# Issuing the second mixing stage of a two-layer trunk in emission order

## The chip, the cores and the metric

One core of a Trainium2 chip runs the kernel. The time is device microseconds of one execution, the median of several; the profile is of one execution more, taken by the hardware profiler.

## What is computed

A trunk of two layers over 272 positions (16 learned ones ahead of 256 of the input) with 2048 features, in float32. Each layer mixes over positions and then runs a gated feed-forward block; a norm ends it.

```python
for layer in range(DEPTH):
    hn = rmsnorm(h, norm_mix_g[layer])
    if layer % 2 == 0:      # linear recurrence + differential attention
        mix = jnp.concatenate([ya, yb], axis=-1) @ ev_w_out[j]
    else:                   # state-space layer + RWKV-7 time mixing
        u, dcols = z[..., :S5_WIDTH], z[..., S5_WIDTH:]
        mix = jnp.concatenate([yc, yd], axis=-1) @ od_w_out[j]
    h = h + mix
    h = h + swiglu(rmsnorm(h, norm_ffn_g[layer]), ...)
return rmsnorm(h, final_norm_g)[:, N_META:]
```

The change touches the second layer's mixing. Its RWKV-7 part is a recurrence over positions in 16 heads of 64 features: per position the state is decayed, corrected by a rank-one term and extended by a new one. The kernel computes it in blocks of 64 positions, two heads at a time (a pair), and needs per block the inverse of triangular matrices of 16 x 16.

## The kernel before

**The dense stream.** All weights are read once, as pieces of up to 8 chunks of 128 x 128. `load_piece_` (line 209) takes a buffer `st` of the pool `wst` (three buffers), starts its load on the sync queue, lets ScalarE cast it to `hi` (line 215) and VectorE compute the rest `lo` (line 216); `whi` and `wlo` have three buffers each. `run_dense` (line 218) walks over the items; each has one or two pieces, an optional `pre`, and an `evac` that empties its PSUM bank. Ahead of a piece's matmuls it emits load and casts of the piece two further on (`ahead=2`). A chunk is three matmuls (lines 249 to 251): `hi` with `xhi`, `hi` with `xlo`, `lo` with `xhi`. After each chunk it calls `tick` (line 104).

**Background work.** `tick` counts chunk steps and advances generators: `s5_states` (the state-space part, one of 32 steps each 13 chunk steps or so, with eight instructions on VectorE), and the pairs of heads, `rwkv` (line 1064). Each `yield n` lets n chunk steps pass before the next part is emitted; all between two yields is emitted in one go. A pair runs in two halves, divided by a bare `yield`: the first prepares its factors and the inverse, the second uses them. Two pairs are under way at most, one in each half: the first half of the next pair starts when the second half of this one has. `rw_finish` emits a pair's remaining parts at once where a later one would overtake its buffers.

**The second mixing stage** is `mix1_items` (line 927): 36 projections of 16 chunks, then the gate of the state-space part (8 items of 8), and the output projection in three passes (16 x 8, 16 x 4, 16 x 4): 896 chunk steps. Projections come per pair as key, receptance, value and one of the state-space input. Their `evac` calls `shift` (line 902): GpSimd clears the first column of `zs` (line 907), VectorE empties the bank into the other columns (line 261), ScalarE scales into `ze` (line 909), and VectorE combines both (line 910). `zs` has two buffers, `ze` one; the state-space input also writes both, and four stores per projection carry them to `s5u`.

**The inverse** in `rwkv`. ScalarE's queue issues the store of the blocks `ld` and later, right ahead of line 1193, four loads `ls` (line 1191) that gather the 16 x 16 blocks. GpSimd inverts them: two clears, then a loop of 15 rounds with a product into `xt` (line 1200) and a sum into `xs` (line 1202). ScalarE's queue issues four stores to `xd` (line 1205) and one load `d16` (line 1207). Loads, inverse and stores are emitted in one go; `yield 34` follows.

**Norm factors.** `head_factors` (line 1291) sums squares with small matmuls (line 1297), scales on VectorE (line 1299), takes a power on GpSimd (line 1300) and spreads the result by a copy on VectorE (line 1302); after a `yield` of 9 (first half) or 8 (second) two or four matmuls (line 1306) use it.

**The order before.** Program order is not issue order: a list scheduler places each instruction on its engine at compile time, by simulated times, taking of those that are ready the one emitted first; casts and evacuations count as 4000 instructions earlier (`hi_pri`). On the chip each engine then keeps that order.

Of the kernel before, what the change touches and what calls it, by code (L numbers as in the profile page):

```python
# [92 lines left out]
class Net:  # L93
# [73 lines left out]
    def setup(self):  # L167
        nc = self.nc
        self.cp = self.pool("cp", 1)
        self.wst = self.pool("wst", 3)  # L170
        self.whi = self.pool("whi", 3)
        self.wlo = self.pool("wlo", 3)
        self.nt = self.pool("nt", 1)
        self.nt2 = self.pool("nt2", 2)
        self.dr = self.pool("dr", 2, space=bass.MemoryType.DRAM)
        self.pd = self.pool("pd", 2, space=bass.MemoryType.PSUM)
        self.bg = self.pool("bg", 1, space=bass.MemoryType.PSUM)
        cp = self.cp
        self.h = self.t(cp, [128, KC, T], "h")
        self.xhi = self.t(cp, [128, KC, T], "xhi", F32R)  # L180
        self.xlo = self.t(cp, [128, KC, T], "xlo", F32R)
        self.vec = self.t(cp, [128, NV], "vec")
        self.ones = self.t(cp, [128, 1], "ones")
        nc.vector.memset(self.ones, 1.0)
# [727 lines left out]
    def mix1_items(self):  # L912
        nc = self.nc
        I = self.I
        st = {}
# [5 lines left out]

        def open_pools():
            es = st["es"] = ExitStack()
            pl = self.m1 = self.pool("m1", 1, es)
            self.m1b = self.pool("m1b", 2, es)
            self.rw = self.load_const("rw", pl)
            V = nc.vector
            self.omu = self.t(pl, [128, 28], "omu")
            V.tensor_scalar(self.omu, self.v("mu"), -1.0, 1.0, op0=ALU.mult, op1=ALU.add)
            self.hv = self.t(pl, [128, 4, 8], "hv")  # L930
            for i, n in enumerate(("w0", "a0", "ka", "glu_b")):
                V.tensor_scalar(self.hv[:, i], self.v(n), 0.5, None, op0=ALU.mult)
            self.oka = self.t(pl, [128, 8], "oka")
            V.tensor_scalar(self.oka, self.v("ka"), -0.5, 1.0, op0=ALU.mult, op1=ALU.add)
            self.lora = {n: self.t(pl, [128, T], "lo_" + n) for n in ("w", "a", "g0", "g1")}
            st["u"] = self.t(pl, [128, 8, T], "u")
            st["y32"] = self.t(pl, [128, 8, TR], "y32")
            st["es2"] = ExitStack()
            self.m2 = self.pool("m2", 1, st["es2"])
            self.m2b = self.pool("m2b", 2, st["es2"])  # L940
            pl = self.m2
            self.ri = [self.t(pl, [128, 4, 2, 64], f"ri{i}") for i in range(2)]
            self.bk = self.t(pl, [128, 5, 3, 64], "bk")
            nc.gpsimd.tensor_copy(self.bk[:, :, 2], self.rw["ist"].unsqueeze(1).to_broadcast([128, 5, 64]))
            for m in self.ri:
                nc.gpsimd.tensor_copy(m[:, :, 1], self.rw["ist"].unsqueeze(1).to_broadcast([128, 4, 64]))
# [43 lines left out]

        def yd_last():
            self.rw_finish(False, 7)
            st["es2"].close()
            pl = self.pool("m3", 1, st["es"])
            st["yd"] = [self.t(pl, [128, 8 - YA, TR], "yd" + n, F32R) for n in "hl"]
            for c in range(YA, 8):
                self.split(st["yd"][0][:, c - YA], st["yd"][1][:, c - YA], st["y32"][:, c])
# [66 lines left out]
    def rwkv(self, p, x, yd):  # L1064
        nc = self.nc
# [69 lines left out]
        def heads(out, lhs, rhs, start=True, stop=True):  # L1135
            for h in range(2):
                e = slice(64 * h, 64 * h + 64)
                PE.matmul(out[e], lhs[e], rhs[e], start=start, stop=stop)  # L1138
# [9 lines left out]
        st = rw["st"]  # L1148
# [41 lines left out]
        for b in range(4):  # L1190
            nc.scalar.dma_start(ls[10 * b:10 * b + 10], bass.AP(tensor=ld.tensor, offset=ld.offset + 1040 * b,
                                                              ap=[[4096, 10], [64, 16], [1, 16]]))
        xs = self.t(pl, [40, 16, 16], "xs")
        xt = self.t(pl, [40, 16, 16], "xt")
        G.memset(xs, 0.0)
        G.memset(F(xs)[:, 0:256:17], 1.0)
        for s in range(15):
            j, n = s + 1, 15 - s
            o = xt[:, :j, :n]
            G.tensor_tensor(o, ls[:, s + 1:, s].unsqueeze(1).to_broadcast([40, j, n]),  # L1200
                            xs[:, :j, s:s + 1].to_broadcast([40, j, n]), op=M)
            G.tensor_tensor(xs[:, :j, s + 1:], xs[:, :j, s + 1:], o, op=A)  # L1202
        xd = self.dr.tile([10, 4, 256], F32, tag="xd", name="xd")
        for b in range(4):
            nc.scalar.dma_start(xd[:, b], F(xs[10 * b:10 * b + 10]))
        d16 = self.t(pl, [128, 5, 16], "d16")
        nc.scalar.dma_start(d16, bass.AP(tensor=xd.tensor, offset=xd.offset, ap=[[16, 128], [2048, 5], [1, 16]]))
        yield 34
        yield
        lg = self.t(pl, [128, 2, 128], "lg")  # L1210
        nc.sync.dma_start(lg, self.I["w_lora"][p, :, 2:4])
# [45 lines left out]
        for c in range(4):  # L1257
            stt = self.t(pb, [128, 64], "stt")
            o = 256 + 64 * (c % 2)
            S.activation(stt, q[:, o:o + 64], AF.Copy, scale=pc[:, c:c + 1])  # L1260
            yield 2
            if c < 3:
                o = 576 - o
                heads(q[:, o:o + 64], kq[:, c, 1], vb[:, c + 1], True, False)
                heads(q[:, o:o + 64], ma[:, c, 1], stt, False, True)
            o = 64 * c
            heads(q[:, o:o + 64], vb[:, c + 1], kq[:, c, 0], True, False)
            heads(q[:, o:o + 64], stt, ma[:, c, 0], False, True)
        ys = self.t(pl, [128, TR], "ys")
        yield 1  # L1270
        S.copy(ys, q[:, :TR])
        yield 2

        q = self.ps("e")
        PE.matmul(q[:, :TR], rw["cen"], ys, start=True, stop=True)
        sq = self.t(pl, [128, 4, 2, 64], "ma").rearrange("p a b c -> p (a b c)")
        S.activation(sq[:, :TR], q[:, :TR], AF.Square)
        S.activation(ys, q[:, :TR], AF.Copy, scale=self.v("ln_w", p))
        yield 3
        yield from self.head_factors(sq[:, :TR], TR, 1.0 / 64, 64e-5, A, "e",  # L1280
                                     self.t(pl, [128, 2, 128], "ie2"), "iv2", 8)
        o = yd[:, p]
# [159 lines left out]
```

## Time and profile before

| | us |
|---|---|
| median of 3 runs | 2596.49 |
| lowest, highest | 2596.41, 2600.54 |
| the profiled execution | 2599.46 |
| its span, first to last instruction | 2597.7 |
| TensorE busy in it | 2519.6 |
| VectorE busy | 1677.8 |
| ScalarE busy | 1167.0 |
| GpSimd busy | 446.4 |

The stages follow each other in the span: the first mixing up to about 420 us, its feed-forward block up to 1240, the second mixing from 1240 to 1812, its feed-forward block and the output. In the profile PE is TensorE, PEld its weight loads, DVE VectorE, ACT ScalarE, POOL GpSimd; L1202 is line 1202. A tile's name stands without its buffer's number. A matmul's duration overlaps the next one's start, so the pace is read from counts over time, not from durations. The share of the clock that is granted is a mean over a stretch: 1.00 is the upper level, 2.4 GHz, and 0.50 the lower, 1.2 GHz.

### The profile page before, as it was taken

To read this page: it belongs to the slowest core of one execution; us is meant where nothing else is said; L and a number is where in the kernel's file an instruction comes from. 1 tells how busy PE (TensorE), PEld (TensorE's weight loads), DVE (VectorE), ACT (ScalarE), POOL (GpSimd) and SP (SyncE) were. 2 spreads that over 40 slices of the span, in tenths; PEclk is the share of its full clock that TensorE was granted. 3 is DMA by queue.
4 is the path that set the end of the run, shared out by engine and by line. 5 is a ranking of instruction groups with operands and counts; after the bars stand their busy time and mean duration, and the time that the engine had idled before them with its cause. 6 is when DMAs were issued, how large, how long until landed. Compare 5 with 4: busy or idle time off the path is not lost.

```text
span 2597.7 us, 52298 instructions
## 1 busy us (share of the span) xinstructions
PE 2519.6 (97%) x21152; PEld 2445.9 (94%) x21152; DVE 1677.8 (65%) x2716; ACT 1167.0 (45%) x1983; POOL 446.4 (17%) x660
## 2 busy tenths in 40 slices
PE   7999999999999999999998999999999999999997
PEld 7999999999999999999887888789999999999997
DVE  7666868787555555557788888656655555555555
ACT  5555646488333333335433333434544434343434
POOL 3111302100001010102133333520210101010103
PEclk9999999999999999999999999999999999999999
DMA  5444456767655555555554544334565566555654
GB/s 188 141 146 141 151 175 202 227 216 254 207 176 173 175 175 172 177 172 184 183 165 137 160 143 139 91 115 147 171 187 180 186 187 187 187 185 184 185 187 145
DMA packets 164546, 448.41 MB, mean 173 GB/s; under 512 B 39313, under 2 KB 55377, under 8 KB 164049
## 3 DMA queue, kind: packets, MB, share of 16 engines
q1 hardware_dynamic: 147728, 442.77, 54.4%
q10 hardware_dynamic: 16576, 2.30, 0.5%
q8 instruction: 167, 2.74, 0.4%
q14 instruction: 75, 0.61, 0.1%
HBM read 422.14 MB, written 22.87 MB: 171 GB/s over the span
## 4 chain that ended last, share of the span: by engine, by line
PE 81%; DVE 5%; DMA 5%; POOL 4%; issue 2%; ACT 1%; ACTq 1%; SPq 0%; DVEq 0%; POOLq 0%
PE p L251 25%; PE p L249 25%; PE p L250 25%; POOL xt L1200 2%; POOL xs L1202 2%; DVE lo L216 2%; DMA ld<-lf 1%; PE b L1138 1%; DMA s5u<-ze 1%; DMA ls<-ld 1%; ACT hi L215 1%; PE a L519 1%; DVE xlo L275 0%; PE c L548 0%; PE a L1138 0%
## 5 line engine op out<-in xcount | busy, mean ns | idle before, releaser
L215 ACT CAST hi<-st 128x1024 fp32r<-128x1024 f32 (+1 forms) x776 | 793.2, 1023 | 1129.9 <-PE p L250 767.6
L216 DVE TENSOR_TENSOR lo<-st,hi 128x1024 fp32r<-128x1024 f32 (+1 forms) x776 | 929.9, 1199 | 521.0 <-ACT hi L215 517.3
L249 PE MATMUL p<-xhi,hi 128*128 128x272 f32 (+1 forms) x4256 | 1236.5, 291 | 15.0 <-ACT hi L215 11.2
L251 PE MATMUL p<-xhi,lo 128*128 128x272 f32 (+1 forms) x4256 | 1235.2, 290 | 8.6 <-DVE lo L216 8.4
L250 PE MATMUL p<-xlo,hi 128*128 128x272 f32 (+1 forms) x4256 | 1231.9, 289 | 0.0
L249 PEld LDWEIGHTS p<-xhi,hi 128*128 128x128 f32 x4256 | 811.5, 191 | 26.1 <-ACT hi L215 13.2
L251 PEld LDWEIGHTS p<-xhi,lo 128*128 128x128 f32 x4256 | 811.7, 191 | 18.7 <-DVE lo L216 10.7
L250 PEld LDWEIGHTS p<-xlo,hi 128*128 128x128 f32 x4256 | 809.9, 190 | 4.5 <-issue 2.4
L251 PE MATMUL p<-ah,lo 128*128 128x272 f32 (+1 forms) x1408 | 401.9, 285 | 0.4 <-DVE lo L216 0.4
L249 PE MATMUL p<-ah,hi 128*128 128x272 f32 (+1 forms) x1408 | 401.0, 285 | 0.4 <-ACT hi L215 0.4
L250 PE MATMUL p<-al,hi 128*128 128x272 f32 (+1 forms) x1408 | 400.9, 285 | 0.0
L356 POOL TENSOR_TENSOR ga<-ga,rb 128x272 f32<-128x272 f32 (+1 forms) x88 | 127.6, 1450 | 1226.6 <-ACT ga L355 1226.6
L251 PEld LDWEIGHTS p<-ah,lo 128*128 128x128 f32 x1408 | 265.8, 189 | 0.7 <-DVE lo L216 0.7
L249 PEld LDWEIGHTS p<-ah,hi 128*128 128x128 f32 x1408 | 265.6, 189 | 0.7 <-ACT hi L215 0.7
L250 PEld LDWEIGHTS p<-al,hi 128*128 128x128 f32 x1408 | 264.8, 188 | 0.0
L265 DVE TENSOR_TENSOR h<-p,h 128x256 f32<-128x256 f32 (+1 forms) x272 | 117.0, 430 | 135.8 <-PE p L251 134.6
L302 POOL TENSOR_TENSOR acc<-acc,sq 128x272 f32<-128x272 f32 (+1 forms) x56 | 59.5, 1063 | 268.8 <-ACT sq L297 268.3
L365 DVE TENSOR_TENSOR gu<-p,ga 128x272 f32<-128x272 f32 (+1 forms) x88 | 38.1, 433 | 61.2 <-PE p L251 58.3
L354 DVE TENSOR_TENSOR ga<-p,rb 128x272 f32<-128x272 f32 (+1 forms) x88 | 38.1, 432 | 51.9 <-PE p L251 51.4
L1200 POOL TENSOR_TENSOR xt<-ls,xs 40x15 f32<-40x15 f32 (+7 forms) x120 | 52.5, 438 | 57.1 <-DMA ls<-ld 48.5
L275 DVE SCALAR_TENSOR_TENSOR xlo<-h,vec,xhi 128x272 fp32r<-128x272 f32 (+1 forms) x64 | 52.1, 823 | 0.3 <-ACT xhi L274 0.3
L1202 POOL TENSOR_TENSOR xs<-xs,xt 40x15 f32<-40x15 f32 (+7 forms) x120 | 47.6, 397 | 8.8
(357 smaller groups left out, 2268.8 us busy)
## 6 DMA issues: line engine op xcount, KB each, us to landing
st<-in_w_gate SPq DMA_DIRECT2D x176, 512.0 KB
st<-in_w_up SPq DMA_DIRECT2D x176, 512.0 KB
st<-in_w_down SPq DMA_DIRECT2D x160, 512.0 KB
st<-in_w_ev_in SPq DMA_DIRECT2D x80, 512.0 KB
st<-in_w_od_in SPq DMA_DIRECT2D x72, 512.0 KB
st<-in_w_ev_out SPq DMA_DIRECT2D x32, 512.0 KB
stab<-s5p SPq DMA_DIRECT2D x32, 400.0 KB
s5p<-stb SPq DMA_DIRECT2D x8, 1088.0 KB
```

The lines of the kernel that those rows point to most:

```text
L215: nc.scalar.copy(hi[:, :kc], st[:, :kc])
L216: nc.vector.tensor_tensor(lo[:, :kc], st[:, :kc], hi[:, :kc].bitcast(F32), op=ALU.subtract)
L249: nc.tensor.matmul(p[:, :n], hi[:, o + k], xa, start=kk == 0, stop=False)
L250: nc.tensor.matmul(p[:, :n], hi[:, o + k], xb, start=False, stop=False)
L251: nc.tensor.matmul(p[:, :n], lo[:, o + k], xa, start=False, stop=kk == tot - 1)
L265: self.nc.vector.tensor_tensor(self.h[:, m, c0:], p, self.h[:, m, c0:], op=ALU.add)
L275: nc.vector.scalar_tensor_tensor(lo, src, g, hi.bitcast(F32), op0=ALU.mult, op1=ALU.subtract)
L302: nc.gpsimd.tensor_tensor(self.acc[:, c0:], self.acc[:, c0:], sq[:, c0:], op=ALU.add)
L354: nc.vector.tensor_tensor(a[:, :n], p, self.rb[:, :n], op=ALU.mult)
L356: nc.gpsimd.tensor_tensor(a[:, :n], a[:, :n], self.rb[:, :n], op=ALU.mult)
L1200: G.tensor_tensor(o, ls[:, s + 1:, s].unsqueeze(1).to_broadcast([40, j, n]), xs[:, :j, s:s + 1].to_broadcast([40, j, n]), op=M)
L1202: G.tensor_tensor(xs[:, :j, s + 1:], xs[:, :j, s + 1:], o, op=A)
```

## The change

`open_pools`, run ahead of the first projection, opens a region in which TensorE, VectorE, ScalarE and GpSimd each issue their instructions in the order in which the program emits them, the DMA issues on ScalarE's queue with them. `yd_last`, run ahead of the last pass of the output projection, closes it. The sync queue, and the order across engines, stay with the scheduler. In `rwkv` the loads of the blocks, the inverse, the stores and the load of `d16` are now emitted 4, 23 and 4 chunk steps apart, with 4 behind (35 in place of 34), and some yields of the second half grow from 2 or 3 to 4. The pool of incoming weights gets a fourth buffer.

```diff
--- before.py
+++ after.py
@@ -167,7 +167,7 @@
     def setup(self):
         nc = self.nc
         self.cp = self.pool("cp", 1)
-        self.wst = self.pool("wst", 3)
+        self.wst = self.pool("wst", 4)
         self.whi = self.pool("whi", 3)
         self.wlo = self.pool("wlo", 3)
         self.nt = self.pool("nt", 1)
@@ -921,6 +921,8 @@
 
         def open_pools():
             es = st["es"] = ExitStack()
+            st["order"] = self.tc.manual_schedule(engines={nc.tensor.engine, nc.vector.engine, nc.scalar.engine, nc.gpsimd.engine})
+            st["order"].__enter__()
             pl = self.m1 = self.pool("m1", 1, es)
             self.m1b = self.pool("m1b", 2, es)
             self.rw = self.load_const("rw", pl)
@@ -990,6 +992,7 @@
 
         def yd_last():
             self.rw_finish(False, 7)
+            st["order"].__exit__(None, None, None)
             st["es2"].close()
             pl = self.pool("m3", 1, st["es"])
             st["yd"] = [self.t(pl, [128, 8 - YA, TR], "yd" + n, F32R) for n in "hl"]
@@ -1190,6 +1193,7 @@
         for b in range(4):
             nc.scalar.dma_start(ls[10 * b:10 * b + 10], bass.AP(tensor=ld.tensor, offset=ld.offset + 1040 * b,
                                                               ap=[[4096, 10], [64, 16], [1, 16]]))
+        yield 4
         xs = self.t(pl, [40, 16, 16], "xs")
         xt = self.t(pl, [40, 16, 16], "xt")
         G.memset(xs, 0.0)
@@ -1200,12 +1204,14 @@
             G.tensor_tensor(o, ls[:, s + 1:, s].unsqueeze(1).to_broadcast([40, j, n]),
                             xs[:, :j, s:s + 1].to_broadcast([40, j, n]), op=M)
             G.tensor_tensor(xs[:, :j, s + 1:], xs[:, :j, s + 1:], o, op=A)
+        yield 23
         xd = self.dr.tile([10, 4, 256], F32, tag="xd", name="xd")
         for b in range(4):
             nc.scalar.dma_start(xd[:, b], F(xs[10 * b:10 * b + 10]))
+        yield 4
         d16 = self.t(pl, [128, 5, 16], "d16")
         nc.scalar.dma_start(d16, bass.AP(tensor=xd.tensor, offset=xd.offset, ap=[[16, 128], [2048, 5], [1, 16]]))
-        yield 34
+        yield 4
         yield
         lg = self.t(pl, [128, 2, 128], "lg")
         nc.sync.dma_start(lg, self.I["w_lora"][p, :, 2:4])
@@ -1258,7 +1264,7 @@
             stt = self.t(pb, [128, 64], "stt")
             o = 256 + 64 * (c % 2)
             S.activation(stt, q[:, o:o + 64], AF.Copy, scale=pc[:, c:c + 1])
-            yield 2
+            yield 4
             if c < 3:
                 o = 576 - o
                 heads(q[:, o:o + 64], kq[:, c, 1], vb[:, c + 1], True, False)
@@ -1269,14 +1275,14 @@
         ys = self.t(pl, [128, TR], "ys")
         yield 1
         S.copy(ys, q[:, :TR])
-        yield 2
+        yield 4
 
         q = self.ps("e")
         PE.matmul(q[:, :TR], rw["cen"], ys, start=True, stop=True)
         sq = self.t(pl, [128, 4, 2, 64], "ma").rearrange("p a b c -> p (a b c)")
         S.activation(sq[:, :TR], q[:, :TR], AF.Square)
         S.activation(ys, q[:, :TR], AF.Copy, scale=self.v("ln_w", p))
-        yield 3
+        yield 4
         yield from self.head_factors(sq[:, :TR], TR, 1.0 / 64, 64e-5, A, "e",
                                      self.t(pl, [128, 2, 128], "ie2"), "iv2", 8)
         o = yd[:, p]
```

## Rows read from the trace of the kernel before

**Rows 1.** page section 1: busy us (share of the span) x instructions, all engines

```profile
PE 2519.6 (97%) x21152; PEld 2445.9 (94%) x21152; DVE 1677.8 (65%) x2716; ACT 1167.0 (45%) x1983; POOL 446.4 (17%) x660
```

**Rows 2.** stretches: from:to us, length, each engine's busy us (x instructions), clock, DMA

```profile
core 0: us, PE busy (x) PEld busy (x) DVE busy (x) ACT busy (x) POOL busy (x), PEclk, DMA share, GB/s
600.00:1200.00 600.00, 600.00 (x4761) 600.00 (x4760) 332.32 (x419) 255.71 (x367) 50.59 (x40) 1.00 0.59 185
420.00:600.00 180.00, 172.16 (x1337) 170.21 (x1337) 148.64 (x303) 118.51 (x275) 19.25 (x12) 0.99 0.71 219
1240.00:1812.00 572.00, 532.72 (x5150) 479.31 (x5149) 429.05 (x747) 208.68 (x414) 181.08 (x414) 0.95 0.47 141
1240.00:1370.00 130.00, 116.89 (x1015) 106.25 (x1015) 102.52 (x171) 45.59 (x80) 35.09 (x77) 0.95 0.56 172
1430.00:1620.00 190.00, 177.65 (x1790) 157.86 (x1789) 158.56 (x280) 65.43 (x133) 66.03 (x163) 0.96 0.50 151
1620.00:1812.00 192.00, 184.10 (x1860) 167.74 (x1860) 117.95 (x212) 78.49 (x161) 56.16 (x124) 0.96 0.37 112
```

**Rows 3.** waits, 1240 to 1812: total us, times, longest

```profile
ACT ze L909 <- DMA s5u<-ze: 21.8, 5, 5.9
...
ACT hi L215 <- DMA xd<-xs: 19.0, 2, 9.9
...
ACT stt L1260 <- DMA xd<-xs: 9.7, 1, 9.7
```

**Rows 4.** timeline near 1516, ScalarE, then TensorE: start, us, engine, line [idle before]

```profile
1516.43 1.43 ACTq L1205 DMA_DIRECT2D xd<-xs  x4
1517.96 1.04 ACT L215 CAST hi<-st 128x1024 fp32r<-128x1024 f32 x1 [9.07 <-DMA xd<-xs]
...
1520.11 0.61 PE L1297 MATMUL e<-c_base,ma 128*128 128x2 f32 x4 [3.44 <-ACT ys L1278]
```

**Rows 5.** timeline of GpSimd: the first, third, sixth, eighth inverse

```profile
1307.72 0.75 POOL L1200 TENSOR_TENSOR xt<-ls,xs 40x15 f32<-40x15 f32 x1 [1.03 <-DMA ls<-ld]
...
1318.58 0.09 POOL L907 MEMSET zs<- 128x1 f32 x1
...
1429.86 0.21 POOL L1200 TENSOR_TENSOR xt<-ls,xs 40x15 f32<-40x15 f32 x1 [6.44 <-DMA ls<-ld]
...
1619.79 0.72 POOL L1200 TENSOR_TENSOR xt<-ls,xs 40x15 f32<-40x15 f32 x1 [4.32 <-DMA ls<-ld]
...
1721.30 0.21 POOL L1200 TENSOR_TENSOR xt<-ls,xs 40x15 f32<-40x15 f32 x1 [6.07 <-DMA ls<-ld]
...
1733.58 0.24 POOL L1202 TENSOR_TENSOR xs<-xs,xt 40x15 f32<-40x15 f32 x1
```

**Rows 6.** chain of work near 1500: start, us, what

```profile
1498.48 2.87 DMA ls<-ld
```

**Rows 7.** groups by shape, 1240 to 1812: shapes, count, busy us, mean ns

```profile
L216 DVE TENSOR_TENSOR lo<-st,hi 128x1024 fp32r<-128x1024 f32 x95 | 118.1, 1243 | 54.9 <-ACT hi L215 54.9
L875 DVE TENSOR_TENSOR_SCAN sz<-s_rho,sx 128x272 f32<-128x272 f32 x64 | 46.4, 752 | 0.0
L876 DVE TENSOR_TENSOR sp<-sz,stab 128x512 f32<-128x512 f32 x64 | 44.5, 719 | 0.0
L868 DVE TENSOR_TENSOR sx<-c,stab 128x544 f32<-128x544 f32 x64 | 44.2, 714 | 1.2 <-PE c L866 1.2
...
L871 DVE TENSOR_TENSOR sx<-sx,sx 128x272 f32<-128x272 f32 x32 | 15.4, 481 | 0.0
...
L870 DVE TENSOR_TENSOR sx<-sx,sx 128x272 f32<-128x272 f32 x32 | 15.0, 468 | 0.2
...
L910 DVE SCALAR_TENSOR_TENSOR rkv<-zs,vec,ze 128x272 f32<-128x272 f32 x24 | 11.9, 497 | 4.0 <-ACT ze L909 4.0
...
L1302 DVE COPY ie<-iv 128x256 f32<-128x256 f32 x8 | 3.5, 444 | 3.8 <-POOL iv L1300 3.8
...
L1300 POOL TENSOR_TENSOR iv<-iv,mhalf 128x4 f32<-128x4 f32 x8 | 11.3, 1416 | 61.4 <-DVE iv L1299 61.3
```

## The prediction

> **What bounds the kernel now.** First the page's busy times: TensorE is busy for 97% of the span [rows 1], so an edit can gain only what TensorE loses. Second the table by stage: in the feed-forward stretch from 600 to 1200 TensorE has no idle microsecond, 4761 matmuls in 600 us, 0.126 us each [rows 2]. The change touches the second mixing stage, 1240 to 1812. There TensorE is busy for 532.7 of 572 us, and the granted clock is 0.95 [rows 2]: part of the stretch is spent at the lower of the two levels, 1.2 instead of 2.4 GHz. Lost are 39 us of idleness and about 0.05 x 572 = 29 us of clock, 68 us in all: the most that ordering can give back. The stage feeds 896 chunk steps (one step: three dense matmuls, 0.38 us); without the losses a step costs (532.7 - 29) / 896 = 0.56 us, background matmuls included.
>
> Third, what the idle time waits for. In the waits of this stage ScalarE stands for up to 10 us at a time before the store of the block inverse `xd` [rows 3]. The timeline shows one such jam: the four issues of line 1205 come at 1516.43, the weight cast behind them had waited 9.07 us, and TensorE stood 3.44 us for a copy in the same queue [rows 4]. The scheduler had put the issue ahead of the inverse's real end. These jams are what the set waits can cure.
>
> Fourth, VectorE: from 1430 to 1620, where the three inner inverses begin at 1429.86 and the sixth at 1619.79 [rows 5], three pairs of heads take 190 us, 63.3 us each, with VectorE busy for 158.6 us, 52.9 us a pair, and TensorE 59 us, about 56 us without the clock's loss [rows 2]. VectorE has 10 us of air per pair and no more.
>
> **The change, part by part.**
>
> *The set waits at the inverse.* With 4, 23, 4 and 4 steps, and the one that follows, the issue of `xd` comes 23 steps (13 us at 0.56) after the inverse's start. The inverse is 30 dependent GpSimd instructions and took 12.5 us from 1721.30 to 1733.82 [rows 5]. The jam goes: I credit 35 of the 39 us of idle time, the rest being entry and exit. Pair 5 is an exception: the call that finishes older pairs at step 544 takes its 23-step wait away, so there the change does not do what it says and the store still holds ScalarE for most of one inverse. I charge it no more than its neighbours, since by (b) VectorE is held at the same time.
>
> *Emission order on GpSimd.* This is where I see a new cost. The loop of lines 1197 to 1202 yields nowhere, so all 30 instructions stand in one block, and whatever is emitted later on GpSimd waits until the last. Before, the scheduler slipped short ones in between: the clear of `zs` (line 907) ran at 1318.58 inside the inverse that began at 1307.72 [rows 5]. Two kinds of work are behind it now.
>
> (a) The power in `head_factors`. Counting yields: from its step A1, a pair issues `ls` after 3+9+8+9+6+4 = 39 steps and the inverse after 43. The second half of the pair before starts 4 steps ahead of A1 and reaches its last power after 2+2+4+15+8+16+1+4+4 = 56, so at 52: 9 steps behind the inverse. The two matmuls that need the result (line 1306) follow 8 steps later, at 60, and TensorE is now held to that order. From the issue of `ls` to there TensorE has 21 steps, 21 x 0.56 = 11.8 us. Against it stand 1.1 us to the last of the four issues (three quarters of the 1.43 us that four such take [rows 4]), 2.9 us from there until GpSimd starts [rows 6], the inverse at 12.5 to 14.5 (12.5 as measured when quiet, 14.5 with two microseconds for VectorE's company), the power 1.4 and the copy 0.44 [rows 7]: 18.3 to 20.3 us. TensorE stands 6.5 to 8.5 us, six times (the inverses of pairs 2 to 7 each meet a predecessor).
>
> (b) The clear of `zs`. `shift` clears one column on GpSimd, and its last VectorE instruction (line 910) reads it. A projection whose result falls inside an inverse therefore parks VectorE until the inverse ends, and the weights' `lo` halves are queued behind it. By the count of steps this happens right at the start for pairs 2, 3, 4 and 5 (inverses at steps 304, 383, 462, 541, projections at 304, 384, 464, 544). Pair 2 worked through: the inverse starts 4.0 us after `ls` is due, 4 steps (2.3 us) being gone, so it ends 1.7 + 14.5 = 16.2 us behind step 304. Two pieces of weights are split ahead, so TensorE runs 16 steps, 9.0 us. The next `lo` is there at 16.2 + 0.5 + 1.24 = 17.9 [rows 7]: TensorE stands 8.9 us. Behind that `lo` are one state-space step (2 x 0.71 + 0.48 + 0.47 + 2 x 0.75 + 2 x 0.72 = 5.3 us), another `lo` of 1.24, then the power and the copy, 8.4 us in all [rows 7]; line 1306 waits for these, one step (0.56) being done meanwhile: 8.9 + 7.8 = 16.7 us in place of 6.5 to 8.5.
>
> How far (b) counts is the open point. If VectorE is already behind when it meets the wait, as its 10 us of air suggest, part of the 16 us is backlog and no loss. By VectorE alone a pair would take 52.9 + 11 to 16 = 64 to 69 us, by TensorE 56 + 16.7 = 72.7, against 63.3. I take 70, nearer to the TensorE row because two waits follow each other on it: +7 for each of four pairs, 28 us. The last two pairs have no projections left and pay (a) alone: 2 x 7.5 = 15, of which the 8 us that TensorE idles there now, 1620 to 1812 [rows 2], give back some 3: +12. The first two pairs, 1240 to 1370, lose 13 us of idle time today [rows 2] and about 8 after (their inverses delay a gelu and one shift each by some 4 us): -5. Stalls of similar number leave the clock's loss as it is.
>
> The inverse's own length depends on VectorE. Unhindered steps took 0.21 us, while the same stretches hold single ones of 0.7 us [rows 5]. On this the Trainium skill (SBUF — State Buffer, "Who interferes with whom") says that a VectorE instruction with two SBUF inputs and a GpSimd instruction that reads SBUF take turns on shared ports, the later one blocking fully. It would mean that a parked VectorE lets the inverse run at its quiet 12.5 us, and (a) and (b) would each shrink by 2 us a pair; the sum by it would be some 12 us lower. The sum above goes without it.
>
> *The longer yields in the second half* (2 to 4 four times, 2 to 4, 3 to 4) add 11 steps to a half that has 79 steps to run in; it ends at step 785 at the latest, before step 832 where it is needed. Nothing.
>
> *The high priority of casts and evacuations* no longer acts in the stage. A cast stands two pieces ahead, 16 steps or 9 us, which covers a queue of one state-space step plus one `lo` (6.5 us). Its price appears only where that cover is gone, in (b).
>
> *The fourth buffer* lets a load start one piece (3 us) earlier. Outside the stage TensorE idles 7.8 us between 420 and 600 [rows 2], the only place with heavy loads beside the weights. Between 0 and -5; I take -2, since the splits, which keep three buffers, still follow TensorE. The sync queue is not ordered and keeps its place.
>
> **Sum.** +28 + 12 - 5 - 2 = +33 us. The profiled execution took 2599.46 us (span 2597.7); the median of the three runs is 2596.49. On the median: 2630 us.
>
> **The rivals.**
>
> *The order simply works* (faster). If VectorE's queue sets the pace, a step costs 52.9 / 78 = 0.68 us or more, and 21 steps last over 14 us; with a quiet inverse of 12.5 us the wait (a) falls to 4 us, and (b) is backlog. Then the 35 us of jams and perhaps 20 of the clock's 29 come back, less 6 x 4 = 24: 2596 - 31 = 2565. It decides from the point where TensorE reaches line 1306 later than the copy is done. Against it: between inverses the last two pairs have VectorE at 118 of 192 us [rows 2], so nothing slows TensorE there. Chance 0.20.
>
> *The waits change places* (no change). Only (a) costs, 6 x 7.5 = 45, plus 8 at the first pairs, against 39 of idle time, with 8 to 20 of the clock's loss back: 2590 to 2602. Chance 0.10.
>
> *A buffer's store holds ScalarE* (slower still). `ze` has one buffer, and ScalarE waited 21.8 us in five places until the stores to `s5u` had read it [rows 3]; in order, each also holds the casts behind. If these come on top, 5 x 4 = 20 us, and (b) counts whole, 4 x (72.7 - 63.3) = 38: 2596 + 20 + 38 + 12 - 5 - 2 = 2659. It decides from the point where the stores take longer than the 16 steps (9 us) to the next projection. Chance 0.20.
>
> *Forecast as summed*: 2630, own range 2610 to 2650. Chance 0.50.
>
> **How the numbers follow.** The range takes in the no-change case, half of the faster one and the slower one with 17 us of clock on top: 2572 to 2676; some 0.1 lies below, 0.06 above. About 0.2% (5 us) is what a measurement of this kernel can tell from no change. Faster by more: 0.21; within: 0.08; slower by more: 0.71.
>
> **What would show it.** Right: the waits name VectorE's copy of `ie` (line 1302) and line 910 as waiting for GpSimd, with each inverse one unbroken run of 30 instructions; TensorE idles once or twice per pair before line 1306 and line 251; the waits for `xd` on ScalarE are gone except at pair 5. Wrong: TensorE idle under 30 us in the stage, or pairs spaced under 60 us, would mean that VectorE's backlog covers the inverse; long waits before line 909 would point to the last rival. Most easily wrong is (b), worked through on one pair and scaled to four.

## Result, and the profile after

The changed kernel takes **2799.5 us** (median; 2798.3 to 2801.8), the kernel before 2596.8 on the same chip: a ratio of 1.0778, interval 1.076 to 1.0797. It is 203 us slower. The forecast was +33 us, its range ended at 2676: the sign was right, the size far off. Lines from the middle of `rwkv` on have numbers 3 to 6 higher in the changed kernel (1138 became 1141, 1205 became 1210, 1213 became 1219, 1239 became 1245, 1302 became 1308, 1306 became 1312).

The page's first section, and from the second the rows of TensorE and its clock in 40 slices of the span:

```profile
PE 2566.8 (92%) x21152; PEld 2478.3 (89%) x21152; DVE 1681.7 (60%) x2716; ACT 1167.8 (42%) x1983; POOL 416.0 (15%) x660
...
PE   8999999999999999986776776678999999999998
...
PEclk9999999999999999998788888889999999999999
```

TensorE fell from 97% [rows 1] to 92%, with the same number of instructions, and all of it in slices 18 to 28. The stretches (columns as in [rows 2]); the second mixing stage now ends near 2010 in place of 1812:

```profile
420.00:600.00 180.00, 176.38 (x1376) 174.94 (x1375) 150.01 (x306) 120.71 (x279) 23.41 (x13) 0.99 0.71 226
600.00:1240.00 640.00, 637.58 (x5061) 636.90 (x5059) 359.24 (x457) 272.94 (x394) 61.74 (x50) 1.00 0.58 183
1240.00:2010.00 770.00, 575.17 (x5105) 507.12 (x5106) 431.07 (x742) 208.02 (x409) 147.19 (x421) 0.85 0.34 104
```

Against the stage's 572 us of before [rows 2], 198 us more. TensorE's idle time went from 39 to 195 us (+156), and about as many matmuls (5105, before 5150) kept it busy for 575 in place of 533 us (+42): the granted clock fell from 0.95 to 0.85, so more of the stage ran at 1.2 GHz. VectorE did the same work (431 us, before 429) and now stood idle for 339 us, before 143. Both are more idle than before, so neither is the bound by its amount of work. Of VectorE's idle time, 139 us ended on ScalarE, 102 on TensorE and 90 on GpSimd.

What TensorE waits for in that stretch (total us, times, longest):

```profile
PE e L1312 <- DVE ie L1308: 51.1, 5, 15.0
PE b L1141 <- DVE z L1245: 38.8, 12, 7.3
PE b L1141 <- DVE dm L1219: 28.4, 8, 9.5
PE e L1303 <- ACT ys L1284: 16.3, 1, 16.3
...
PE p L251 <- DVE lo L216: 8.1, 2, 7.4
```

Then what VectorE, and ScalarE, wait for there:

```profile
DVE rkv L910 <- POOL zs L907: 37.4, 3, 13.3
...
DVE rkv L910 <- ACT ze L909: 26.7, 20, 12.6
DVE ie L1308 <- POOL iv L1306: 25.3, 8, 10.0
DVE u L640 <- ACT gl L639: 24.1, 8, 5.2
```

```profile
ACT ze L909 <- DVE zs L261: 125.3, 22, 18.2
...
ACT ze L909 <- DMA xd<-xs: 17.9, 1, 17.9
...
ACT ze L909 <- DMA s5u<-ze: 7.6, 1, 7.6
```

The two waits that the forecast priced are there: the copy `ie`, 51 us on TensorE, and line 910 behind GpSimd, which shows on TensorE as the wait for `lo`, 8.1 us. But 910 meets an inverse three times, not four, and the next two lines of TensorE's list, 67 us for `z` and `dm` in 20 places, stand in no term of the forecast. The jam behind the store `xd` is left at one place, pair 5, as foreseen; there ScalarE stood for 17.9 us and TensorE for 16.3 (the wait for `ys`).

One place where the predicted chain can be read off, in the timeline of VectorE (start, us, engine, line, operation, idle time before):

```profile
1502.32 0.44 DVE L261 TENSOR_TENSOR zs<-p,rb 128x272 f32<-128x272 f32 x1 [1.65 <-PE p L251]
1516.04 0.50 DVE L910 SCALAR_TENSOR_TENSOR rkv<-zs,vec,ze 128x272 f32<-128x272 f32 x1 [13.28 <-POOL zs L907]
1516.45 1.22 DVE L216 TENSOR_TENSOR lo<-st,hi 128x1024 fp32r<-128x1024 f32 x1
1517.59 1.35 DVE L868 TENSOR_TENSOR sx<-c,stab 128x544 f32<-128x544 f32 x2
...
1522.40 1.22 DVE L216 TENSOR_TENSOR lo<-st,hi 128x1024 fp32r<-128x1024 f32 x1
1523.54 0.15 DVE L1305 TENSOR_SCALAR iv<-e 128x4 f32<-128x4 f32 x1
1524.84 0.31 DVE L1308 COPY ie<-iv 128x256 f32<-128x256 f32 x1 [1.15 <-POOL iv L1306]
```

and of TensorE, first the matmuls that make the input of `iv` (durations min/median/max, first and last start), then its two stalls:

```profile
L1303 PE MATMUL e<-c_base,ma x4: 167/251/252, 1506.9 to 1507.1; 128*128 128x2 f32 x4
```

```profile
1517.73 0.59 PE L251 MATMUL p<-xhi,lo 128*128 128x272 f32 x1 [7.35 <-DVE lo L216]
1525.30 1.19 PE L1312 MATMUL e<-c_base,ie 128*128 128x128 f32 x4 [6.98 <-DVE ie L1308]
```

This is mechanism (b) with nearly its predicted price: stalls of 7.35 and 6.98 us, worked out as 8.9 and 7.8. That the first is so near is partly luck: the inverse took 10.7 us in place of the 14.5 assumed, but it began later and TensorE ran dry sooner. The place also shows what the forecast didn't generalize. The 0.15 us instruction `iv` had its input from 1507.35 (the last start, 1507.1, and 0.25 us) and ran at 1523.54, 16 us later, behind an instruction that waited and a block that nobody needed yet.

It happens without an inverse too. Some 45 us on, while GpSimd runs none, VectorE does one block after another, and between them stands `z`:

```profile
1562.69 1.23 DVE L216 TENSOR_TENSOR lo<-st,hi 128x1024 fp32r<-128x1024 f32 x1 [0.51 <-ACT hi L215]
1563.83 1.35 DVE L868 TENSOR_TENSOR sx<-c,stab 128x544 f32<-128x544 f32 x2
...
1568.04 0.69 DVE L876 TENSOR_TENSOR sp<-sz,stab 128x512 f32<-128x512 f32 x1
1568.64 0.69 DVE L1245 TENSOR_TENSOR z<-b,z 128x512 f32<-128x512 f32 x1
```

```profile
1558.93 1.09 PE L1141 MATMUL b<-z,gt 64*64 64x128 f32 x16
1569.38 1.97 PE L1141 MATMUL b<-rbt,z 64*64 64x128 f32 x16 [7.28 <-DVE z L1245]
```

The input of `z` was complete at 1560.02; `z` ran 8.6 us later, behind a weight half and a state-space step, and TensorE stood for 7.28 us of it. From such pairs of rows I worked out how long a ready VectorE instruction stood, from the last matmul that could feed it to its start, summed over the stage:

| VectorE instruction | before | changed | changed, VectorE back to the scheduler |
|---|---|---|---|
| `iv` from TensorE's `e`, 8 times | 17.9 us | 50.2 us | 4.8 us |
| `z` from TensorE's `b`, 24 times | 35.0 us | 65.5 us | 18.8 us |
| `iv` from TensorE's `a`, 8 times | 16.9 us | 22.7 us | 5.6 us |

### The profile page after: what moved, and what is told of

It is laid out like the page before. It is cut to its first block, busy times and chain, and to the rows that moved or that the text cites. A ratio compares the mean times of both kernels' runs of the same rounds, so it can differ in the third digit from the quotient of the medians.

```text
span 2797.5 us, 52294 instructions
## 1 busy us (share of the span) xinstructions
PE 2566.8 (92%) x21152; PEld 2478.3 (89%) x21152; DVE 1681.7 (60%) x2716; ACT 1167.8 (42%) x1983; POOL 416.0 (15%) x660
## 4 chain that ended last, share of the span: by engine, by line
PE 78%; DVE 8%; issue 4%; POOL 4%; ACT 3%; DMA 3%; ACTq 0%; SPq 0%; DVEq 0%; POOLq 0%
PE p L249 24%; PE p L251 23%; PE p L250 23%; DVE lo L216 2%; PE b L1141 2%; PE a L1141 1%; POOL xt L1204 1%; POOL xs L1206 1%; ACT hi L215 1%; DVE sx L868 1%; DVE sz L875 1%; DMA ls<-ld 1%; POOL iv L1306 1%; DVE sp L876 1%; PE a L519 1%
## 5 line engine op out<-in xcount | busy, mean ns | idle before, releaser
L249 PE MATMUL p<-xhi,hi 128*128 128x272 f32 (+1 forms) x4256 | 1261.4, 296 | 11.2 <-ACT hi L215 9.1
L251 PE MATMUL p<-xhi,lo 128*128 128x272 f32 (+1 forms) x4256 | 1235.4, 290 | 16.6 <-DVE lo L216 16.3
L909 ACT ACTIVATE ze<-zs,omu 128x272 f32<-128x272 f32 x28 | 14.6, 522 | 151.8 <-DVE zs L261 125.3
L354 DVE TENSOR_TENSOR ga<-p,rb 128x272 f32<-128x272 f32 (+1 forms) x88 | 38.0, 432 | 51.9 <-PE p L251 50.2
L1204 POOL TENSOR_TENSOR xt<-ls,xs 40x15 f32<-40x15 f32 (+7 forms) x120 | 40.5, 337 | 115.0 <-DMA ls<-ld 106.2
L1312 PE MATMUL e<-c_base,ie 128*128 128x128 f32 x32 | 7.8, 386 | 51.1 <-DVE ie L1308 51.1
```

The source lines that it names most:

```text
L249: nc.tensor.matmul(p[:, :n], hi[:, o + k], xa, start=kk == 0, stop=False)
L251: nc.tensor.matmul(p[:, :n], lo[:, o + k], xa, start=False, stop=kk == tot - 1)
L354: nc.vector.tensor_tensor(a[:, :n], p, self.rb[:, :n], op=ALU.mult)
```

## Experiments

The letters in the expectations, as far as they are used: A, GpSimd's unbroken inverse as in the forecast; B, an engine's emission order is dear by itself, VectorE's above all, because it holds ready work behind an instruction that waits; C, a convoy, in which each in-order engine is late only because the others answer at fixed places; D, distance: a pair's first half has too few steps for its chain; F, the casts come too late without their priority. All runs compute everything.

### The change taken apart: buffer alone, yields alone

```
e1_buffer, on the kernel before:   self.wst = self.pool("wst", 4)
e2_yields, on the kernel before:   the diff's yields, and nothing else
```

> The kernel before with one edit: four buffers for incoming weights in place of three, no other part of the change. Theory A (the unbroken inverse on GpSimd holds the other engines) and theory B (VectorE's queue in emission order delivers too late for TensorE) both say that the buffer has nothing to do with the 203 us: 2592 to 2597 us, the feed-forward stretch between 420 and 600 us losing up to 5 of its 7.8 us of idle TensorE. A result above 2605 would mean that the extra load ahead takes bandwidth from the state-space loads.

> The kernel before with the yields of the change alone: 4, 23, 4 and 4 chunk steps around the inverse and the longer ones in the second half; three buffers, no region of emission order. Both theories: the scheduler keeps its freedom, so no stall of the changed kernel appears; 2580 to 2605 us. If the yields themselves were the harm (a second half that ends too late), it would be over 2650.

The buffer alone: 2591.8 us, ratio 0.998 (0.997 to 0.9991), 5 us gained; TensorE's busy time between 420 and 600 rose from 172.2 [rows 2] to 176.1 us. The yields alone: 2596.9 us, 0.9993 (0.9982 to 1.0005), nothing; ScalarE still waits for the store `xd`, 16.5 us in two casts and 8.2 in one copy, since the scheduler places the issue where it likes. So the loss belongs to the emission order, and the yields don't move an issue unless its engine is in order.

### One engine out of the order

```
e3_pe_free, e4_dve_free, e5_pool_free, e6_act_free: in open_pools
- manual_schedule(engines={nc.tensor.engine, nc.vector.engine, nc.scalar.engine, nc.gpsimd.engine})
+ manual_schedule(engines={ ... without that one engine})
e11_dve_pool_free: without VectorE and GpSimd
```

> The changed kernel with TensorE left to the scheduler; VectorE, ScalarE and GpSimd in emission order. VectorE's results are as late as before in simulated time too, so the scheduler puts dense matmuls ahead of matmuls that would wait. If TensorE's held order turns lateness into stalls (theory B needs that), 100 to 180 us come back: 2620 to 2700 us. If lateness of VectorE and GpSimd in itself sets the pace (their chains being longer than the stage), under 60 come back: 2740 or more.

> The changed kernel with VectorE left to the scheduler (casts and evacuations early again, steps of the state-space part interleaved with the pairs' short instructions); TensorE, ScalarE and GpSimd in emission order. Theory B: the waits of TensorE for z (39 us), dm (28 us), sp, re and ma (22 us) mostly go, and with their share of the clock the time falls by 90 to 140 us, to 2660 to 2710. Theory A: VectorE's order is not the cause; the waits for ie stay, under 50 us come back, 2750 or more.

> The changed kernel with GpSimd left to the scheduler; TensorE, VectorE and ScalarE in emission order. Theory A: the clears and powers slip ahead of the inverse or into it, the waits for the copy ie (51 us), for ys behind pair 5's inverse (16 us) and for lo (16 us) go, and with a third of the clock's loss the time falls by 90 to 120 us, to 2680 to 2710. Theory B: powers depend on VectorE, which is still late; at most 40 us come back, 2760 to 2800.

> The changed kernel with ScalarE left to the scheduler; TensorE, VectorE and GpSimd in emission order. ScalarE waits long in the changed kernel (125 us before the scaling into ze, for VectorE), but it is busy for 208 of 770 us. Theory C: its answers to VectorE come earlier when it may pass a waiting instruction; 30 to 80 us back, 2720 to 2770. Theory B: under 20 us.

> The changed kernel with VectorE and GpSimd left to the scheduler; TensorE and ScalarE in emission order. If the two engines' orders are separate causes, the gains of 104 and 33 us add: about 2660. If GpSimd's block is what remained in the run with VectorE free (50 us of waits for ie, 16 for pair 5), more: 2600 to 2630. What stays above 2597 is the price of ScalarE's and TensorE's order.

| engine given back to the scheduler | us | of the 203 |
|---|---|---|
| TensorE | 2790.5 | -9 |
| GpSimd | 2766.7 | -33 |
| ScalarE | 2749.6 | -50 |
| VectorE | 2695.2 | -104 |
| VectorE and GpSimd | 2677.4 | -122 |

GpSimd, the one queue that carried the forecast's loss, is worth 33 us, a sixth of what was lost, where theory A wanted 90 to 120. That this equals the +33 of the forecast is chance: the forecast's stalls came to 4 x 16.7 + 2 x 7.5 = 82 us, and the +33 is what stayed after credits. VectorE is half of the loss, within theory B's 90 to 140; ScalarE's 50 lie in theory C's range and not in B's. VectorE and GpSimd together give 122, less than the 137 of the two apart, and some 80 us over the kernel before stay with TensorE and ScalarE alone in order. TensorE gives back 9, where 100 to 180 were expected if its held order made the stalls. TensorE's waits with VectorE free (1240 to 2010):

```profile
PE e L1312 <- DVE ie L1308: 49.6, 5, 11.0
PE e L1303 <- ACT ys L1284: 15.9, 1, 15.9
PE b L1141 <- DVE dm L1219: 10.4, 5, 3.6
```

`ie`, which waits for the power behind GpSimd's inverse, stays at 50 us; `z` leaves the list and `dm` falls from 28 to 10. This speaks for two causes, the forecast's mechanism for `ie` and VectorE's own order for `z` and `dm`, but the runs do not part them cleanly. With GpSimd free, `ie` only halves (24.8 us in 4) and `dm` rises to 37.3; with ScalarE free, `ie` falls further (17.4 in 4); with VectorE and GpSimd both free, `dm` is back at 27.8. With TensorE free its waits only move, to `lo` (60.1 us in 30 at line 251) and `hi` (38.8 in 16).

### One engine alone in the order

```
f1_only_vector, f2_only_scalar, f3_only_tensor: in open_pools
+ manual_schedule(engines={ ... that one engine})
```

> The changed kernel with VectorE alone in emission order; TensorE, ScalarE and GpSimd go to the scheduler again. Theory B (VectorE's emission order is dear by itself: it does a pair's bursts and state-space groups unbroken, whoever waits): 2650 to 2700, since taking VectorE out of the order gave 104 us back. Theory C (a convoy: each in-order engine is late only because the others answer at fixed places): under 2630, much less than the 104 us. In both the waits of TensorE for VectorE's `z` and `dm` (line 1141) lead the list if the kernel is slower than before by over 40 us.

> The changed kernel with ScalarE alone in emission order. Theory B: ScalarE's order costs what taking it out gave back, 50 us: about 2640. Theory C: 2590 to 2615, since VectorE, out of the order, answers early. The wait behind the store `xd` at pair 5 (16 us of TensorE in the changed kernel) stays in both.

> The changed kernel with TensorE alone in emission order. Taking TensorE out of the order gave 9 us back. Theory B: 2600 to 2610, TensorE's order costs next to nothing anywhere. Theory C: 2610 to 2660, since a TensorE bound to the emission order waits for whatever the scheduler has put late on the other engines, and the 9 us were small only because the others were bound too. Theory D: as C, with the waits on the pair's first half (lines 1303 to 1312 and 1141).

VectorE alone: 2732.5 us (1.0509, 1.0479 to 1.054), **+133**. ScalarE alone: 2689.8 (1.0345), +90. TensorE alone: 2645.5 (1.0175), +46. Each is dear by itself, and all three beyond what B gave them: theory C, by which VectorE's order would have cost some 30 us at most alone, falls as the explanation of VectorE's and ScalarE's price, while TensorE's 46 us fit C's range and not B's. GpSimd alone in order was not run. The three sum to 269, more than the 203 of all four, so the prices are not parts of one sum; that the waits overlap is the likely reason, not shown. Nor does TensorE always wait in the same place. With VectorE alone in order:

```profile
PE p L251 <- DVE lo L216: 38.8, 25, 4.3
PE c L866 <- DMA us<-s5u: 23.3, 6, 4.8
PE e L1303 <- ACT ys L1284: 12.0, 4, 5.4
PE e L1312 <- DVE ie L1308: 10.0, 6, 2.7
PE b L1141 <- DVE z L1245: 7.9, 8, 2.0
```

`z` and `dm` do not lead, against what I had expected: the scheduler now places TensorE's matmuls, and the stall shows at the next thing that VectorE owes, the weights. By the measure of the table above, `iv` from `a` now stood ready for 146.3 us and `z` for 45.8, while `iv` from `e` (17.0) stood no longer than in the kernel before. With TensorE alone in order its waits are spread: `sp` of the state-space part 20.1 us in 7 places, `z` and `ie` 13.7 each. With ScalarE alone in order the jam of the kernel before comes back in full, now at 65 us: the inverse runs where the scheduler puts it while the issue keeps its place in ScalarE's queue, and all eight stores are issued within 0.1 us of the end of their inverse. TensorE now waits for the casts (`hi`, 34.3 us in 12 places); its 16 us behind the store of pair 5, expected to stay, are down to 1.7.

```profile
ACT hi L215 <- DMA xd<-xs: 65.4, 6, 13.0
```

### Smaller blocks in emission order

```
e7_inverse_parts, in the inverse's loop:   yield 2 if s < 8 else 1   (in place of yield 23 behind it)
e8_state_parts:   yields between the VectorE instructions of a state-space step, groups of 2, 2, 4, 5
e9_both_parts:    both
e10_round_trips:  e9, and yields that part round trips between engines in gelu2, head_factors
                  and the scans; line 910 and the split of u issued two steps later
```

> The changed kernel with the inverse emitted round by round, two chunk steps apart for eight rounds and one apart for seven (23 in all, as before): clears and powers emitted meanwhile stand between the rounds. Theory A, as corrected by the run with GpSimd free (33 us): 2735 to 2770, the waits for ie and the 37 us of VectorE's wait for the clear of zs mostly gone. Theory A as first put: 2680 to 2710. Theory B: the same 2735 to 2770, with z and dm untouched.

> The changed kernel with each state-space step's eight VectorE instructions (5.3 us in one burst) emitted in four groups, 2, 2, 4 and 5 chunk steps apart, 13 in all as before. Theory B: the short results that TensorE waits for (z, dm, ma, re) no longer stand behind 5.3 us but behind 1.5 at most: 60 to 100 us come back, 2700 to 2740. Theory A: under 20 us, 2780 or more.

> Both: the inverse round by round and the state-space steps in four groups, in emission order on four engines. If the two causes are separate, the gains add: 2640 to 2700 us. If one hides the other (VectorE parked by the clear is what makes its queue late), the gain exceeds the sum of the two single ones.

> On top of the inverse in rounds and the state-space steps in groups, the round trips are parted: wherever VectorE's next instruction waits for ScalarE or GpSimd to answer an instruction emitted in the same go (the power in head_factors, the gelu, the scan in the pair's first part, the factor of its keys, the shift of a projection, the split of the state-space input), 2 or 3 chunk steps of other emission now lie between. Theory C (in emission order VectorE stands still at the head of its queue for these answers, 280 us of waits in the run with both parts, and delivers z and dm late for that reason): 70 to 120 us come back against that run, 2630 to 2680 us. Theory B (VectorE's amount of work in bursts): under 30 us, 2720 or more.

2768.8, 2767.1, 2747.9 and 2738.2 us: -31, -32, -52 and -61. Breaking the inverse gives 31 us, about the 33 that GpSimd's freedom gives, so that price is the unbroken block. The state-space block on VectorE is as dear, and half or less of what I expected; the two together give less than their sum, and less than the 2640 to 2700 expected. Parting every round trip I could find adds some 10, with intervals that overlap (1.0572, 1.0528 to 1.0615, and 1.0535, 1.0514 to 1.0556), where theory C wanted 70 or more. After this last edit VectorE waits for casts of ScalarE, and ScalarE again for the store, now that the inverse is spread out:

```profile
DVE lo L219 <- ACT hi L218: 148.3, 85, 18.5
```

```profile
ACT ze L928 <- DMA xd<-xs: 37.1, 4, 16.2
```

A block that is cut ends later, and what was placed by counting steps behind it is then too early.

### Distance, priority, and the lead of the casts

```
f4_first_half_longer, on the changed kernel: yields 3 to 6, 9 to 13 and 8 to 15 in the first half
                                             of rwkv; two of 3 to 2, and 23 to 20
g1_no_priority, on the kernel before:        hi_pri() does nothing in the second mixing stage
g2_casts_earlier, on the changed kernel:     run_dense(..., ahead=3); wst 3, whi 4, wlo 4 buffers
```

> The changed kernel, all four engines in emission order, with 14 chunk steps more between the start of a pair's normalizing factors and its inverse (yields 3 to 6, 9 to 13 and 8 to 15; two yields of 3 to 2 and the wait of 23 to 20 give part of it back, so a pair takes some 85 steps in place of 79). Theory D (the chain needs some 28 us and the emission order gives it 20 steps, 11 us at 0.56): the waits for `dm` and `z` (line 1141) and for `ie` shrink from 118 us to under 70 and the time falls by 30 to 60 us, to 2740 to 2770. Theory B (VectorE's order is dear by itself, whatever the distances): within 15 us of the changed kernel, 2785 to 2815. A longer pair can also push the last pairs out of the stage: then slower, with TensorE waiting at its end.

> The kernel before, with the high priority of casts, evacuations and loads taken away in the second mixing stage, everything else to the scheduler as before. Theory F (the lost priority is what the emission order costs): 40 to 150 us slower, 2640 to 2750, with TensorE waiting for `lo` at line 251. Theory B (only the fixed order costs, the scheduler finds the casts' places without it): within 15 us of before.

> The changed kernel with casts three pieces ahead of TensorE in place of two (four buffers of `hi` and `lo`, three of the raw weights): 24 steps of lead in place of 16, everything still in emission order. Theory F: the time falls by 40 us or more, to under 2760. Theory B: within 15 us of the changed kernel (2785 to 2815), since in the changed kernel TensorE waits only some 16 us for `lo` and over 130 us for results of the pairs' own chains.

Fourteen more steps for the chain of the first half: 2804.0 us, ratio 1.0784, which is not to be told from the changed kernel's 1.0778. In its waits `ie` shrinks from 51 to 14 us and `z` from 39 to 23, but `dm` grows from 28 to 44 and others take their place:

```profile
PE b L1141 <- DVE dm L1219: 43.6, 6, 9.6
PE e L1294 <- DVE ys L1289: 32.1, 5, 16.0
PE b L1141 <- DVE z L1245: 22.8, 10, 6.2
PE c L887 <- DVE sp L876: 22.6, 6, 5.8
```

Theory D falls: the three waits that it names shrink from 118 to 81 us (it wanted under 70), and the time doesn't move. The kernel before without any priority in the stage: 2592.3 us, ratio 0.9974 (0.9957 to 0.9992), not slower at all. The changed kernel with casts three pieces ahead: 2802.8 us, ratio 1.0793, no gain. Theory F falls from both sides.

### The jams off ScalarE's queue

```
e12_store_gpsimd, on the kernel before: wst 4 buffers; the stores of xd (line 1205) and the load of
d16 (line 1207) issued by nc.gpsimd in place of nc.scalar
```

> The kernel before with four buffers for weights, and the stores of the inverse and the load that follows them issued by GpSimd, which makes the inverse, in place of ScalarE; no region of emission order. If the jams of ScalarE's queue behind these stores are the idle time of the stage before, as the prediction said, some 20 us of TensorE's idleness and 10 of the clock's loss go: 2560 to 2575 us. If GpSimd's issues are slow and hold its queue as long, no change: 2588 to 2597.

2590.9 us, ratio 0.9965 (0.9951 to 0.9979), where the buffer alone has 0.998 (0.997 to 0.9991): the intervals overlap, and no gain beyond the buffer's is shown. That is the second branch of the expectation, and the trace shows why. No wait of ScalarE for `xd` is left, but the jam has moved with the issues. GpSimd stands idle before the load `d16`, which needs the stores, and a power is queued behind it; VectorE waits for the power, and TensorE for VectorE (rows of GpSimd and VectorE, then TensorE's list):

```profile
1518.04 0.91 POOL L1207 DMA_DIRECT2D d<-xd  x1 [5.16 <-issue]
...
1519.41 1.04 POOL L1300 TENSOR_TENSOR iv<-iv,mhalf 128x4 f32<-128x4 f32 x1
...
1520.48 0.77 DVE L1302 COPY ie<-iv 128x256 f32<-128x256 f32 x1 [10.88 <-POOL iv L1300]
```

```profile
PE e L1306 <- DVE ie L1302: 10.2, 1, 10.2
PE b L1138 <- DVE dm L1213: 8.6, 2, 6.8
```

TensorE's idle time in 1240 to 1812 is 44 us, with the jams 39 to 43 (kernel before, buffer alone). So this run doesn't show what the jams cost, since it puts new stalls in their place; no run removes them alone. The timeline of the kernel before gives a measure. Within 6 us of each of the first seven stores of `xd` a stall of TensorE ends, of 5.25, 2.43, 2.60, 3.44, 3.62, 3.96 and 1.68 us; the first, the fifth and the sixth:

```profile
1331.51 0.79 PE L866 MATMUL c<-us,stab 128*128 128x272 f32 x2 [5.25 <-DVE rkv L910]
...
1575.71 0.48 PE L1275 MATMUL e<-ys,c_rw 128*128 128x256 f32 x1 [3.62 <-ACT ys L1271]
...
1636.07 0.48 PE L1138 MATMUL e<-kq,vb 64*64 64x64 f32 x4 [3.96 <-ACT stt L1260]
```

The first waits for VectorE, which stood behind the late cast, the other six for ScalarE. They sum to 23.0 of the 39 us; that all of it would go with the jams is not shown. This kernel, the buffer alone and the one without priorities are the only versions faster than the kernel before, by 0.2 to 0.35%.

## Why the prediction was wrong in size

*What bounds the kernel*: right, and it should have been a warning. A stage in which TensorE idles 39 of 572 us has 68 us to win and no bottom on the other side.

*The set waits at the inverse* (35 us credited): the mechanism was right, the credit too large. ScalarE's waits for `xd` went but for pair 5, foreseen with its cause. But the credit took nearly all of TensorE's idle time as the jams', on one timeline in which a jam of 9.07 us cost TensorE 3.44 [rows 4]. The stalls right behind the stores come to 23.0 of the 39 us, so some 12 of the 35 had no ground; how much of the 23 would have come back stays open, since the one run without these jams on ScalarE had them on GpSimd.

*Emission order on GpSimd* ((a) and (b), +28 and +12): right in kind, and nearly in size as far as stalls go. Each inverse is one unbroken run, `ie` heads TensorE's list and 910 stands behind `zs`. The stalls priced came to 82 us; the waits of those kinds (`ie` 51.1, `lo` 8.1, `ys` at pair 5 16.3) to 75.5. But giving GpSimd back returns only 33 us and breaking the inverse 31: other waits end behind these.

*The step that failed* is the sentence on priority, "Its price appears only where that cover is gone, in (b)", and what it stood for: VectorE, ScalarE and TensorE in emission order were costed at nothing outside the reach of an inverse. Of TensorE's 195 us of idleness, over 100 lie in waits that no term priced, `z` and `dm` first. The cover of the casts was sufficient as far as the runs show (priority removed alone, no loss; a third piece of lead, no gain), so the sentence was right about the casts and asked about the wrong thing. Its premise, that only GpSimd has work stuck in order, was false. VectorE's order costs 133 us alone and 104 in company, ScalarE's 90 and 50, TensorE's 46 and 9. The profile of before had the hint: VectorE is busy for 52.9 us in a pair's 63.3, and I read this as "10 us of air", a stock of slack. In emission order each wait at the head of its queue takes from that air, and over the changed stage it idled 339 us.

*The clock* ("Stalls of similar number leave the clock's loss as it is"): consistent in itself, but the stalls were not of similar number. 195 us of idleness came with 0.85 in place of 0.95, 42 us of longer matmuls. The rival's range had 17 us for it.

*The longer yields*: nothing, as said (0.9993). *The fourth buffer*: -2 taken, -5 the bound, -5 measured. *The rivals*: the one with the store of `ze` and (b) whole, 2659, was nearest in time and wrong in its reason: ScalarE waits for `s5u` in one place, 7.6 us, before in five, 21.8 us [rows 3]. That the order simply works is out.

*The rule on the shared ports* (the Trainium skill, SBUF — State Buffer, "Who interferes with whom") agrees with the trace. Here are two of the same step of the inverse, one beside VectorE's `sp` (two inputs in SBUF, 0.69 us from 1425.24), one while VectorE stood still before line 910:

```profile
1425.41 0.69 POOL L1206 TENSOR_TENSOR xs<-xs,xt 40x64 f32<-40x64 f32 x1
...
1510.63 0.31 POOL L1206 TENSOR_TENSOR xs<-xs,xt 40x64 f32<-40x64 f32 x1
```

The three inverses beside which VectorE stood still took 10.6 to 10.7 us (the first of them from 1505.31 to 1515.97), the two inverses ahead of them, with VectorE busy for 8 to 9 us, 14.1 and 14.2. So the 12.5 of [rows 5] was not the quiet length, and the 14.5 in (b) was too long; beside the 203 us this matters little.

*What is shown and what is open.* Shown: the loss is the emission order's; no single engine carries it; VectorE's order is the dearest alone and in company; more lead for the casts, their priority and a longer first half give nothing back; GpSimd's block is 31 to 33 us of the loss and the state-space block 32, 52 together. Supported, by ready instructions standing 50 us in place of 18 and 65 in place of 35, and less than before with VectorE freed: VectorE holds ready work behind a head that waits. Open: which placements make up the remaining 140 us of the kernel with all blocks parted, and what the jams before were worth. Each repair shortened the wait it was made for, and the time moved little; an order with TensorE as free of waits as the scheduler's was not found by hand.

## To carry to other kernels

When a region is put into emission order, cost every engine that loses its scheduler, not just the one with the long block: for each in-order queue, list what its head waits for and what stands ready behind it, and do not count the idle time of an engine that feeds the bound as slack (here VectorE, busy for 52.9 of 63.3 us). Before crediting a removed wait with the bound's idle time, add up the stalls that follow that wait: here 23 of 39 us. To move a wait to another queue is not to remove it. And steps counted in the code fix a distance only for engines that are in order; here the issue in order behind a GpSimd that wasn't held casts for 65 us, before for 19.

## What the runs showed of the hardware

TensorE's granted clock fell with its stalls. In the changed stage it idled for 195 of 770 us, the longest stalls 15 to 16 us, and the mean clock was 0.85, so part of the stage ran at the lower level; in the stage before, 39 of 572 us and 0.95; in the feed-forward work from 600 to 1240, 2 of 640 us and 1.00. The stalls were paid a second time: the same matmuls took 42 us longer, on top of 156 us more idleness. A GpSimd step that met a VectorE instruction with two SBUF inputs took 0.69 in place of 0.31 us.
